# The first norm of a hybrid RWKV-7 and pooling trunk: x transposed unscaled, the row factors applied to each projection

## The chip, the cores and the metric

The kernel runs on one core of one Trainium2 chip. TensorE multiplies matrices, VectorE and ScalarE work on tiles of 128 rows, GpSimd does small things beside them, and each has its own queue of instructions that is worked off in order. SyncE issues most of the transfers from and to device memory. Matrix products land in PSUM, from where VectorE or ScalarE read them; everything else lies in SBUF. The metric is device time in microseconds (us), lower is better.

## The reference

There is one layer (DEPTH 1), a sequence of 512 rows and a width of 2048. Cut to what matters here:

```
def rms_norm(x, g):
    y = xf * lax.rsqrt(jnp.mean(xf * xf, axis=-1, keepdims=True) + RMS_EPS)
    return (y * g).astype(x.dtype)

h = rms_norm(x, norm_g[i])
z = jnp.einsum('btd,dn->btn', h, w_in[i])
zs, g_rwkv, u, g_pool = split(z)              # r, k, v, two LoRA inputs | gate | pool input | pool gate
zs = zs + (token_shift(zs) - zs) * mu[i]
w_loglog = -softplus(-(w0[i] + tanh(wd) @ w_up[i])) - 0.5
a = sigmoid(a0[i] + ad @ a_up[i])
y = wkv7_scan(rh, wh, kh, vh, kk, ah)         # the recurrence, 16 heads of 64
y_rwkv = (head_group_norm(y, ln_w, ln_b) + bonus) * silu(g_rwkv)
y_pool = (causal_multiscale_pool(u) @ w_pool) * pool_scale * silu(g_pool)
x = x + concat(y_rwkv, y_pool) @ w_out[i]
x = x + sigmoid(x @ w_pg[i] + b_pg[i]) * (p[i] @ w_ple[i])
return rms_norm(x, final_g)
```

The norm divides each row (each position of the sequence) by a factor of its own and multiplies each column by norm_g. Since the projection is linear, a row's factor may be applied to x or to the row of z.

## The kernel before, in words

Activations are kept transposed: hhi and hlo hold h with the 2048 columns on 16 groups of 128 partitions and the 512 positions along the free axis. All large products are made three times, from a high part and a low part of each operand (`mm3`: high weight with high h, high weight with low h, low weight with high h); a weight chunk of 4 times 128 rows by 128 columns comes in as `raw` (256 KB) and is split by ScalarE (`whi`, L132) and VectorE (`wlo`, L133). A projection of 128 columns (`zcols`) is 48 such products of 512 columns into one PSUM accumulator, of which there are two (`psA`).

The start loads x in row groups of 128: the first two in four pieces each, the third and fourth in halves with the LoRA columns' four weight chunks between them (`LORD`). `stats` squares a row group on ScalarE (L256) and VectorE (L258), takes the root, and multiplies x by it in place (L267, L269). Then `xt_half` transposes two row groups of one group of 128 columns at a time into PSUM (L285) and evicts the result twice: hhi by ScalarE (L286), hlo by VectorE (L287), both with norm_g as the column's factor. That goes over 16 groups of columns for positions 0 to 255, then again for 256 to 511, with the products of `z_half` for zl, the LoRA columns, between the second. WPOS and SPOS say behind which of the groups the LoRA weights are split and the later row groups are normed.

From `pin[0] = True` on TensorE keeps the order in which the program is written. Behind the start come zk, zr, zv and zg of the first head pair. For each of eight head pairs there follow its preparation (scores pm, masked by VectorE at L623) and its recurrence, `recur`: 8 chunks of three steps each, py, pu and ps. py waits for sbd (VectorE, L807 and L809), pu for zs (VectorE, L787), ps for uv (ScalarE, L797). Between the steps `pump` puts 6, 9 and 9 products of the next pair's projections or of the pool's (zb), so that TensorE has work while the other engines answer. VectorE's order is not written out: a scheduler decides it, and zs and sbd have a raised priority in it.

zl goes into `shifted` (L369 and L370) and becomes la, which is copied twice (`dup`, by transfers) and split; `decay_and_rate` multiplies it with the two LoRA matrices of each pair. silu2 (L373 and L374) makes the gates; `pool_unit` copies each pool input out of PSUM (L412). In the names below, `xt` is x, `zk`, `zr`, `zg`, `zb` are accumulators of projections, `bk` and `bkn` come from k, and `prm` holds the small parameters.

Of the kernel before, what the change touches and what calls it, by code (L numbers as in the profile page):

```python
# [9 lines left out]
F32 = mybir.dt.float32  # L10
# [24 lines left out]
def trunk_kernel(ctx: ExitStack, tc: tile.TileContext, x, p, norm_g, w_in, mu, w0, w_up, a0, a_up,  # L35
# [17 lines left out]
    psX = sx.enter_context(tc.tile_pool(name="psX", bufs=3, space=PSUM))  # L53
    xs = []

    def load_x(tt, parts):
        xt = xp.tile([P, D], F32, name=f"xt{tt}", tag="xt")
        w_ = D // parts
        for i in range(parts):
            nc.sync.dma_start(out=xt[:, i * w_:(i + 1) * w_], in_=x[tt * P:(tt + 1) * P, i * w_:(i + 1) * w_])  # L60
        xs.append(xt)
# [168 lines left out]
    def load_l():  # L230
# [2 lines left out]
        nc.sync.dma_start(out=raw, in_=src)  # L233
        lraw.append(raw)

    for step in LORD:
        if step == "l":
            load_l()
        else:
            load_x(step, 2)  # L240
# [6 lines left out]
    WPOS, SPOS = (5, 7, 9, 11), (5, 10)  # L247

    def stats(tt, parts=2):
        w_ = D // parts  # L250
        ss = xp.tile([P, parts], F32, name=f"ss{tt}", tag="ss")
        for i in range(parts):
            cs = slice(i * w_, (i + 1) * w_)
            junk = xp.tile([P, w_], F32, name=f"junk{tt}_{i}", tag=f"junk{i % 2}", bufs=2)
            if i % 2 == 0:
                nc.scalar.activation(junk, xs[tt][:, cs], AF.Square, accum_out=ss[:, i:i + 1])  # L256
            else:
                nc.vector.scalar_tensor_tensor(junk, xs[tt][:, cs], 1.0, xs[tt][:, cs], ALU.mult, ALU.mult,  # L258
                                               accum_out=ss[:, i:i + 1])
        rs = xp.tile([P, 1], F32, name=f"rs{tt}", tag="rs")  # L260
        nc.vector.tensor_reduce(rs, ss, mybir.AxisListType.X, ALU.add)
        nc.scalar.activation(rs, rs, AF.Sqrt, bias=epsr, scale=1.0 / D)
        nc.vector.reciprocal(rs, rs)
        for i in range(4):
            cs = slice(i * D // 4, (i + 1) * D // 4)
            if i % 2 == 1:
                nc.scalar.activation(xs[tt][:, cs], xs[tt][:, cs], AF.Copy, scale=rs)  # L267
            else:
                nc.vector.tensor_scalar(xs[tt][:, cs], xs[tt][:, cs], rs, None, ALU.mult)  # L269

    stats(0, 4)
# [23 lines left out]
    wl_ = []  # L295
    for d in range(KT):
        xt_half(0, d)
        if d in WPOS:
            c = len(wl_)
            wh = wp.tile([P, CK, P], F32R, name=f"whi_l_{c}", tag="whi")  # L300
            wl = wp.tile([P, CK, P], F32R, name=f"wlo_l_{c}", tag="wlo")
            split(wh, wl, lraw[c])
            wl_.append((wh, wl))
        if d in SPOS:
            stats(2 + SPOS.index(d))
    for d in range(KT):
        xt_half(1, d)
        z_half(0, d)
    for d in range(KT):
        z_half(1, d)  # L310
    pt = psM.tile([P, T], F32, name="pt_prm", tag="m")
    nc.tensor.transpose(pt[:, :nr], prow, ident[:nr, :nr])
    nc.vector.tensor_copy(prm, pt[:, :nr])
    sx.close()

# [29 lines left out]
    pin[0] = True  # L345
    wab = {}

    def load_ab(j):
# [14 lines left out]
    nc.gpsimd.memset(uaz[0][64:128, :].bitcast(F32), 0.0)  # L363
    nc.gpsimd.memset(uaz[1][0:64, :].bitcast(F32), 0.0)
    for t_ in sbd + zsp:
        nc.gpsimd.memset(t_, 0.0)

# [11 lines left out]
    lal = rw.tile([P, T], F32R, name="lal")  # L379
    hh = []  # L380
    for nm, rows in (("u", slice(0, 64)), ("a", slice(64, 128))):
        dup = rw.tile([P, T], F32, name=f"dup_{nm}", tag="t", bufs=4)
        for h in range(2):
            nc.scalar.dma_start(out=dup[64 * h:64 * h + 64, :], in_=la[rows, :])
        t_ = rw.tile([P, T], F32R, name=f"{nm}hh")
        nc.scalar.copy(t_, dup)
        nc.vector.tensor_tensor(lal[rows, :], dup[rows, :], t_[rows, :].bitcast(F32), ALU.subtract)
        hh.append(t_)
    uhh, ahh = hh

# [2 lines left out]

    place = [0]

    def zcols(ps, nm):
        for c in range(KT // CK):
            wh, wl = chunk(nm, c)
            for k in range(CK):
                kk = c * CK + k  # L400
                mm3(ps, wh[:, k, :], wl[:, k, :], hhi[:, kk, :], hlo[:, kk, :], kk == 0, kk == KT - 1)
                place[0] = 3 * (kk + 1)
                yield 3

    def pool_unit(n):
        g, i = n // 4, n % 2
        win = WINDOWS[g]
        ps = psA.tile([P, T], F32, name=f"zb{n}", tag="acc")
        yield from zcols(ps, f"b{n}")
# [51 lines left out]
    def stream():  # L461
        for kind, nm, j in jobs:
# [6 lines left out]
            if kind == "p":  # L469
# [49 lines left out]
    def decay_and_rate(j):  # L519

        (ur, us), (ar_, as_) = wab.pop(j)
        for raw, st, z_, lo, hi in ((ur, us, uaz[0], slice(64, 128), slice(0, 64)),
                                    (ar_, as_, uaz[1], slice(0, 64), slice(64, 128))):
# [6 lines left out]
        mm(ps, uaz[0], lal, start=False, stop=True)  # L530
# [650 lines left out]
```

## Time and profile before

| what | value |
| --- | --- |
| time, median of 3 runs | 1096.56 us (1095.4 to 1097.19) |
| span of the profiled execution | 1095.9 us (the page gives no time of it beside the span) |
| TensorE busy | 1070.8 us, 98% of the span |
| TensorE weight loads | 877.6 us, 80% |
| VectorE busy | 708.2 us, 65% |
| ScalarE busy | 448.3 us, 41% |
| GpSimd busy | 76.9 us, 7% |
| mean granted clock | 0.998 of full speed |
| HBM read, written | 118.02 MB, 18.87 MB; 125 GB/s over the span |

The page's strip of 40 slices has TensorE at 9 or more tenths in all slices but the first (5) and the last (6), and VectorE between 5 and 9 until about the 25th slice. A busy TensorE leaves little that a change elsewhere can win, so the stretch ahead of its first full slice, and the few waits behind it, are what the rows below look at.

### The profile page before, as it was taken

To read this page: it belongs to the slowest core of one execution; us is meant where nothing else is said; L and a number is where in the kernel's file an instruction comes from. 1 tells how busy PE (TensorE), PEld (TensorE's weight loads), DVE (VectorE), ACT (ScalarE), POOL (GpSimd) and SP (SyncE) were. 2 spreads that over 40 slices of the span, in tenths; PEclk is the share of its full clock that TensorE was granted. 3 is DMA by queue.
4 is the path that set the end of the run, shared out by engine and by line. 5 is a ranking of instruction groups with operands and counts; after the bars stand their busy time and mean duration, and the time that the engine had idled before them with its cause. 6 is when DMAs were issued, how large, how long until landed. Compare 5 with 4: busy or idle time off the path is not lost.

```text
span 1095.9 us, 17196 instructions
## 1 busy us (share of the span) xinstructions
PE 1070.8 (98%) x6060; PEld 877.6 (80%) x6060; DVE 708.2 (65%) x1835; ACT 448.3 (41%) x917; POOL 76.9 (7%) x180
## 2 busy tenths in 40 slices
PE   5999999999999999999999999999999999999996
PEld 4888878887788888788878788888888888888885
DVE  6687867878688679678886956454433424445366
ACT  7633535345335335353343344543222222233337
POOL 2100110110110110100101101000000000000000
PEclk9999999999999999999999999999999999999999
DMA  7433433332423333333334242775534438455534
GB/s 233 116 96 97 111 92 84 96 100 73 120 82 105 104 92 89 96 82 93 91 94 119 79 138 93 232 233 169 172 124 136 167 99 244 137 189 137 181 106 154
DMA packets 178486, 138.56 MB, mean 126 GB/s; under 512 B 34678, under 2 KB 139743, under 8 KB 178399
## 3 DMA queue, kind: packets, MB, share of 16 engines
q1 hardware_dynamic: 157694, 103.89, 32.1%
q10 hardware_dynamic: 20704, 33.56, 9.8%
q8 instruction: 48, 0.79, 0.3%
q14 instruction: 40, 0.32, 0.1%
HBM read 118.02 MB, written 18.87 MB: 125 GB/s over the span
## 4 chain that ended last, share of the span: by engine, by line
PE 86%; DVE 5%; DMA 4%; ACT 3%; issue 1%; SPq 0%; ACTq 0%; DVEq 0%
PE acc_o L157 16%; PE zb L157 14%; PE acc_g L157 14%; PE zv L157 8%; PE zk L157 7%; PE zg L157 7%; PE zr L157 7%; PE py L157 2%; PE pple L157 2%; PE pm L157 1%; PE pu L157 1%; DMA n<-nd 1%; PE pp L157 1%; DMA raw_g<-in_w_pg_dram 1%; PE ps L157 1%
## 5 line engine op out<-in xcount | busy, mean ns | idle before, releaser
L133 DVE TENSOR_TENSOR wlo_g<-raw_g,whi_g 128x512 fp32r<-128x512 f32 x84 | 57.0, 685 | 79.6 <-ACT whi_g L132 76.5
L157 PE MATMUL zb<-hhi,whi_b 128*128 128x512 f32 x256 | 107.0, 418 | 0.0
L133 DVE TENSOR_TENSOR wlo_o<-raw_o,whi_o 128x512 fp32r<-128x512 f32 x64 | 43.9, 690 | 91.4 <-ACT whi_o L132 91.4
L157 PE MATMUL zb<-hhi,wlo_b 128*128 128x512 f32 x256 | 100.5, 393 | 0.0
L157 PE MATMUL acc_o<-whi_o,ylo 128*128 128x512 f32 x256 | 100.2, 391 | 0.0
L157 PE MATMUL acc_o<-whi_o,yhi 128*128 128x512 f32 x256 | 99.9, 390 | 0.0
L157 PE MATMUL zb<-hlo,whi_b 128*128 128x512 f32 x256 | 99.9, 390 | 0.0
L157 PE MATMUL acc_o<-wlo_o,yhi 128*128 128x512 f32 x256 | 99.8, 390 | 0.0
L132 ACT CAST whi_g<-raw_g 128x512 fp32r<-128x512 f32 x84 | 51.9, 620 | 102.7 <-PE acc_g L157 55.4
L157 PE MATMUL acc_g<-whi_g,x2hi 128*128 128x512 f32 x208 | 81.3, 391 | 0.0
L157 PE MATMUL acc_g<-wlo_g,x2hi 128*128 128x512 f32 x208 | 80.9, 389 | 0.0
L157 PE MATMUL acc_g<-whi_g,x2lo 128*128 128x512 f32 x208 | 80.7, 389 | 0.0
L132 ACT CAST whi_o<-raw_o 128x512 fp32r<-128x512 f32 x64 | 39.9, 623 | 97.0 <-PE acc_o L157 96.7
L816 POOL TENSOR_SCALAR s0p<-sbd,pw 64x64 f32<-64x64 f32 x96 | 56.6, 589 | 322.8 <-DVE sbd L809 255.0
L132 ACT CAST whi_b<-raw_b 128x512 fp32r<-128x512 f32 x64 | 39.7, 621 | 86.5 <-PE zv L157 35.4
L133 DVE TENSOR_TENSOR wlo_b<-raw_b,whi_b 128x512 fp32r<-128x512 f32 x64 | 43.8, 685 | 34.2 <-ACT whi_b L132 32.9
L157 PEld LDWEIGHTS zb<-hhi,wlo_b 128*128 128x128 f32 x256 | 48.0, 188 | 11.1
L661 DVE TENSOR_TENSOR xw<-xw,tm 128x60 f32<-128x60 f32 (+24 forms) x248 | 52.1, 210 | 6.8
L157 PEld LDWEIGHTS acc_o<-wlo_o,yhi 128*128 128x128 f32 x256 | 48.1, 188 | 10.3 <-DVE wlo_o L133 0.4
L157 PEld LDWEIGHTS acc_o<-whi_o,yhi 128*128 128x128 f32 x256 | 48.1, 188 | 9.7
L157 PEld LDWEIGHTS acc_o<-whi_o,ylo 128*128 128x128 f32 x256 | 48.1, 188 | 9.8
L157 PEld LDWEIGHTS zb<-hhi,whi_b 128*128 128x128 f32 x256 | 48.2, 188 | 8.5
(285 smaller groups left out, 2550.0 us busy)
## 6 DMA issues: line engine op xcount, KB each, us to landing
raw_b<-in_w_in_dram SPq DMA_DIRECT2D x64, 256.0 KB
raw_o<-in_w_out_dram SPq DMA_DIRECT2D x64, 256.0 KB
raw_g<-in_w_pg_dram SPq DMA_DIRECT2D x64, 256.0 KB
raw_k<-in_w_in_dram SPq DMA_DIRECT2D x32, 256.0 KB
raw_r<-in_w_in_dram SPq DMA_DIRECT2D x32, 256.0 KB
raw_v<-in_w_in_dram SPq DMA_DIRECT2D x32, 256.0 KB
raw_g<-in_w_in_dram SPq DMA_DIRECT2D x32, 256.0 KB
n<-nd SPq DMA_DIRECT2D x16, 256.0 KB
```

Of the source, the lines that this page charges most:

```text
L132: nc.scalar.copy(hi, raw)
L133: nc.vector.tensor_tensor(lo, raw, hi.bitcast(F32), ALU.subtract)
L157: i = nc.tensor.matmul(*a, **k)
L661: nc.vector.tensor_tensor(xw[:, 0:n_, s + 1:32], xw[:, 0:n_, s + 1:32], tm[:, 0:n_, 0:w_], ALU.add)
L816: nc.gpsimd.tensor_scalar(s0p[hc, :], nxt[hc, hc], pcn[hc], None, ALU.mult)
```

## The change

The row factors no longer multiply x. x is transposed as it lands, the squares are taken beside, and the factors of all 512 positions are laid out as one row repeated over 128 partitions: four diagonal tiles (`dg`) are multiplied by a tile of ones in one fp32 product, and the result (`rsB`, 128x512) multiplies each finished projection in PSUM (`by_row`). The first two weight chunks of zk are multiplied ahead of that product (`k_first`). The loads of x come in another order, and the low parts of the LoRA operands are packed into the unused halves of their tiles.

```diff
-    load_x(0, 4)
+    load_x(0, 0)
     ngr = xp.tile([KT, P], F32, name="ngr", bufs=1)
-    load_x(1, 4)
+    load_x(1, 0)
+    for i in range(1, 4):
+        for tt in range(2):
+            load_x(tt, i)
...
-    LORD = (2, "l", "l", "l", "l", 3)
+    LORD = ("l", 2, 3, "l", 2, 3, "l", "l")
...
-        nc.vector.reciprocal(rs, rs)
-        for i in range(4):
-            cs = slice(i * D // 4, (i + 1) * D // 4)
-            if i % 2 == 1:
-                nc.scalar.activation(xs[tt][:, cs], xs[tt][:, cs], AF.Copy, scale=rs)
-            else:
-                nc.vector.tensor_scalar(xs[tt][:, cs], xs[tt][:, cs], rs, None, ALU.mult)
+    def roots():
+        rs = xp.tile([P, NT, 1], F32, name="rs", bufs=1)
+        nc.vector.tensor_reduce(rs, ssq_, mybir.AxisListType.X, ALU.add)
+        nc.scalar.activation(rs, rs, AF.Sqrt, bias=epsr, scale=1.0 / D)
+        nc.vector.reciprocal(rs, rs)
+        dg = xp.tile([P, NT, P], F32, name="dg", bufs=1)
+        for tt in range(NT):
+            nc.vector.tensor_scalar(dg[:, tt, :], ident, rs[:, tt, :], None, ALU.mult)
+        ps = psM.tile([P, T], F32, name="prs", tag="m")
+        mm(ps, ones, dg.rearrange("p a t -> p (a t)"), start=True, stop=True)
+        nc.scalar.copy(rsB, ps)
...
+    BEGUN = 2
+
+    def k_first(c):
+        wh, wl = ready.pop(("k0", c))
+        for k in range(CK):
+            kk = c * CK + k
+            mm3(begun, wh[:, k, :], wl[:, k, :], hhi[:, kk, :], hlo[:, kk, :], kk == 0, False)
...
     for d in range(KT):
         xt_half(1, d)
+        if d in (1, 5):
+            split_l()
         z_half(0, d)
     for d in range(KT):
         z_half(1, d)
+        if d % CK == CK - 1 and d < 3 * CK:
+            ahead_k()
+        square(d // 4, d % 4)
+    pin[0] = True
+    begun = psA.tile([P, T], F32, name="zk0", tag="acc")
+    for c in range(BEGUN):
+        k_first(c)
+    roots()
...
+    nc.vector.tensor_tensor(zl, zl, rsB, ALU.mult)
     shifted(zl, la, 24)
...
+    def by_row(ps):
+        nc.vector.tensor_tensor(ps, ps, rsB, ALU.mult)
...
                 place[0] = 3 * (kk + 1)
+                if kk == KT - 1 and scaled:
+                    by_row(ps)
                 yield 3
...
-            nc.scalar.copy(u_, ps)
+            nc.vector.tensor_tensor(u_, ps, rsB, ALU.mult)
...
-            nc.scalar.copy(z_[hi, :], raw[hi, :])
-            nc.vector.tensor_tensor(st[lo, :], raw[lo, :], st[lo, :].bitcast(F32), ALU.subtract)
+            nc.vector.tensor_tensor(z_[0:64, :], raw[0:64, :], st[0:64, :].bitcast(F32), ALU.subtract)
```

The first place where the order of the instructions differs is the head of VectorE's queue. Before, it reads as follows (xt_78 is the first group of 128 rows of x, xt_85 the second):

```order
L258 SCALAR_TENSOR_TENSOR junk_1_164,ss_161<-xt_78 128x512
L258 SCALAR_TENSOR_TENSOR junk_3_168,ss_161<-xt_78 128x512
L261 TENSOR_REDUCE rs_170<-ss_161 128x1
L263 RECIPROCAL rs_170<-rs_170 128x1
L269 TENSOR_SCALAR xt_78<-xt_78,rs_170 128x512 x2
L258 SCALAR_TENSOR_TENSOR junk_1_184,ss_181<-xt_85 128x512
L86 CAST blk<-blkf 128x128
L274 COPY ngc<-pt_prm 128x16
L258 SCALAR_TENSOR_TENSOR junk_3_188,ss_181<-xt_85 128x512
L261 TENSOR_REDUCE rs_190<-ss_181 128x1
L263 RECIPROCAL rs_190<-rs_190 128x1
L269 TENSOR_SCALAR xt_85<-xt_85,rs_190 128x512 x2
```

Behind these rows stood the first hlo. In the changed kernel the head of the same queue is this (xt_79 is now the second group of rows; the number behind junk is the quarter of the columns):

```order
L264 SCALAR_TENSOR_TENSOR junk_1_401,ssq__164<-xt_78 128x512
L89 CAST blk<-blkf 128x128
L281 COPY ngc<-pt_prm 128x16
L264 SCALAR_TENSOR_TENSOR junk_3_417,ssq__164<-xt_78 128x512
L264 SCALAR_TENSOR_TENSOR junk_1_427,ssq__164<-xt_79 128x512
L293 SCALAR_TENSOR_TENSOR hlo<-pt_h_0_169,ngc,hhi 128x256
L293 SCALAR_TENSOR_TENSOR hlo<-pt_h_1_174,ngc,hhi 128x256
```

The scalings and roots are gone from the head of the queue, three squares are left ahead of the first hlo.

The second place is TensorE's order between zl and zk. Before, it goes from the last products of zl (and the transposition of the small parameters, prow) to zk:

```order
L157 MATMUL zl<-hlo,whi_l_297 128x256
L157 MATMUL zl<-hhi,wlo_l_298 128x256
L312 MATMUL pt_prm<-ident,prow 128x89
L157 MATMUL zk_595<-hhi,whi_k_0_598 128x512
L157 MATMUL zk_595<-hlo,whi_k_0_598 128x512
```

In the changed kernel the first 24 products of zk stand behind zl, and then, in the middle of zk, the product that makes the row factors (prs):

```order
L163 MATMUL zk_491<-hhi,whi_k_1_439 128x512
L163 MATMUL zk_491<-hlo,whi_k_1_439 128x512
L163 MATMUL zk_491<-hhi,wlo_k_1_440 128x512
L163 MATMUL prs<-dg,ones 128x512
L167 MATMUL pt_prm<-ident,prow 128x89
L163 MATMUL zk_491<-hhi,whi_k_2_465 128x512
```

The transposition of prow moved behind the half of zk, together with prs.

The third place is VectorE's order in the recurrence of the fourth head pair. Before, zs stands behind small steps of a triangular inverse (tm and xw) and ahead of a weight's split:

```order
L661 TENSOR_TENSOR xw4_4761<-xw4_4761,tm4_4762 128x2x27
L657 TENSOR_TENSOR tm4_4762<-xw4_4761,n324_0_4666 128x2x26
L661 TENSOR_TENSOR xw4_4761<-xw4_4761,tm4_4762 128x2x26
L787 TENSOR_TENSOR zs1_569<-py3_0_4568,mv3_4382 64x128
L133 TENSOR_TENSOR wlo_r5_3_2672<-raw_r5_3_2669,whi_r5_3_2671 128x512
```

In the changed kernel the multiplication of the finished projection zk of the sixth pair stands there, and the split behind it:

```order
L688 TENSOR_TENSOR tm4_4750<-xw4_4749,n324_0_4653 128x2x26
L692 TENSOR_TENSOR xw4_4749<-xw4_4749,tm4_4750 128x2x26
L425 TENSOR_TENSOR zk5_4687<-zk5_4687,rsB_112 128x512
L139 TENSOR_TENSOR wlo_r5_3_2716<-raw_r5_3_2713,whi_r5_3_2715 128x512
L818 TENSOR_TENSOR zs1_600<-py3_0_4555,mv3_4368 64x128
```

The multiplication and the split have come ahead of zs, which stood ahead of the split before.

## Rows read from the trace of the kernel before

**Rows 1.** Stretches: bounds, length, busy (count) of five engines, clock, DMA share, GB/s
```profile
10.00:20.00 10.00, 7.66 (x42) 5.96 (x43) 8.12 (x23) 8.90 (x22) 0.00 (x0) 1.00 0.90 291
20.00:30.00 10.00, 8.85 (x67) 7.63 (x67) 9.66 (x25) 9.77 (x24) 0.00 (x0) 1.00 0.38 110
...
400.00:500.00 100.00, 99.13 (x698) 79.99 (x696) 80.84 (x241) 46.03 (x99) 9.36 (x17) 1.00 0.33 90
```
**Rows 2.** Scalings, 0 to 36 us, by form: operation and count | busy, mean ns | idle before
```profile
L269 DVE TENSOR_SCALAR xt<-xt,rs 128x512 f32<-128x512 f32 x8 | 3.5, 483 | 0.1
```
**Rows 3.** VectorE's timeline, 0 to 75 us: start, length, instruction [idle before]
```profile
6.76 0.69 DVE L258 SCALAR_TENSOR_TENSOR junk<-xt 128x512 f32<-128x512 f32 x1 [1.08 <-DMA xt<-in_x_dram]
...
10.55 0.69 DVE L258 SCALAR_TENSOR_TENSOR junk<-xt 128x512 f32<-128x512 f32 x1 [0.54 <-DMA xt<-in_x_dram]
...
13.80 2.44 DVE L287 SCALAR_TENSOR_TENSOR hlo<-pt_h,ngc,hhi 128x256 fp32r<-128x256 f32 x6 [0.84 <-ACT hhi L286]
...
26.25 7.22 DVE L287 SCALAR_TENSOR_TENSOR hlo<-pt_h,ngc,hhi 128x256 fp32r<-128x256 f32 x18
...
39.49 0.75 DVE L370 SCALAR_TENSOR_TENSOR la<-zl,prm,la 128x511 f32<-128x511 f32 x1 [1.43 <-ACT la L369]
...
72.89 0.68 DVE L600 TENSOR_TENSOR bk<-kk,ipw 128x512 f32<-128x512 f32 x1
```
**Rows 4.** TensorE's timeline, 30 to 76 us
```profile
31.63 0.38 PE L285 MATMUL pt_h<-ident,xt 128*128 128x128 f32 x2
...
35.83 0.48 PE L157 MATMUL zk<-hhi,whi_k 128*128 128x512 f32 x1
...
46.82 0.39 PE L157 MATMUL zr<-hhi,whi_r 128*128 128x512 f32 x1
...
75.47 2.06 PE L157 MATMUL pm<-ar,bk 64*128 64x128 f32 x32
```
**Rows 5.** ScalarE's timeline, 0 to 75 us (ACTq issues transfers)
```profile
9.96 0.63 ACT L256 ACTIVATE junk<-xt 128x512 f32<-128x512 f32 x1
...
36.23 1.20 ACTq L354 DMA_DIRECT2D ur<-in_w_up_dram  x2
```
**Rows 6.** TensorE's timeline, six steps of the recurrence
```profile
137.94 0.38 PE L157 MATMUL py<-sbd,ar 128*128 128x128 f32 x2
...
140.15 0.49 PE L157 MATMUL pu<-zs,x 128*128 128x128 f32 x2 [0.44 <-DVE zs L787]
...
144.85 0.38 PE L157 MATMUL py<-sbd,ar 128*128 128x128 f32 x2
...
146.46 0.38 PE L157 MATMUL pu<-zs,x 128*128 128x128 f32 x2
...
148.76 0.38 PE L157 MATMUL ps<-uv,bkn 128*128 128x128 f32 x2
...
151.06 0.38 PE L157 MATMUL py<-sbd,ar 128*128 128x128 f32 x2
```
**Rows 7.** What TensorE waited for, 36 us to the end: us, times, longest
```profile
PE py L157 <- DVE sbd L809: 1.6, 4, 0.9
PE pss L157 <- ACT bkn L700: 0.9, 2, 0.5
...
PE pu L157 <- DVE zs L787: 0.4, 1, 0.4
```
**Rows 8.** All engines, 364.9 to 367 us: one step py to pu
```profile
364.98 0.38 PE L157 MATMUL py<-sbd,ar 128*128 128x128 f32 x2
...
366.36 0.42 PEld L157 LDWEIGHTS pu<-zs,x 128*128 128x128 f32 x2
```
**Rows 9.** VectorE and ScalarE by form, 36 to 700 and to 720 us
```profile
L623 DVE TENSOR_TENSOR mt<-pm,msk 128x512 f32<-128x512 f32 x32 | 19.9, 682 | 0.9 <-PE pm L157 0.8
L133 DVE TENSOR_TENSOR wlo_b<-raw_b,whi_b 128x512 fp32r<-128x512 f32 x58 | 39.6, 685 | 27.6 <-ACT whi_b L132 26.3 <-DMA nd<-mt 0.9 <-issue 0.2
...
L412 ACT COPY u<-zb 128x512 f32<-128x512 f32 x8 | 4.7, 586 | 0.1
```

More of the change, by code (lines that the diff above doesn't have):

```diff
@@ L54, in trunk_kernel, with load_x @@
     xs = []
-    def load_x(tt, parts):
-        xt = xp.tile([P, D], F32, name=f"xt{tt}", tag="xt")
+    for tt in range(NT):
+        xs.append(xp.tile([P, D], F32, name=f"xt{tt}", tag="xt"))
+    def load_x(tt, i, parts=4):
         w_ = D // parts
-        for i in range(parts):
-            nc.sync.dma_start(out=xt[:, i * w_:(i + 1) * w_], in_=x[tt * P:(tt + 1) * P, i * w_:(i + 1) * w_])
-        xs.append(xt)
-    load_x(0, 4)
+        nc.sync.dma_start(out=xs[tt][:, i * w_:(i + 1) * w_], in_=x[tt * P:(tt + 1) * P, i * w_:(i + 1) * w_])
+    load_x(0, 0)
     ngr = xp.tile([KT, P], F32, name="ngr", bufs=1)
     nc.sync.dma_start(out=ngr, in_=norm_g[0].rearrange("(r c) -> r c", c=P))
-    load_x(1, 4)
+    load_x(1, 0)
+    for i in range(1, 4):
+        for tt in range(2):
+            load_x(tt, i)
     epsr = cst.tile([P, 1], F32, name="epsr")
@@ L90, in trunk_kernel @@
     nc.gpsimd.memset(seg.rearrange("p (c t) -> p c t", t=C)[:, :, 0:1], 0.0)
+    ones = xp.tile([P, P], F32, name="ones", bufs=1)
+    nc.gpsimd.memset(ones, 1.0)
+    rsB = cst.tile([P, T], F32, name="rsB")
     msk = cst.tile([P, 3, C], F32, name="msk")
@@ L234, in load_l @@
         lraw.append(raw)
+    halves = []
     for step in LORD:
@@ L239, in trunk_kernel @@
         else:
-            load_x(step, 2)
+            load_x(step, halves.count(step), 2)
+            halves.append(step)
     for n_, src, r_ in names:
@@ L244, in trunk_kernel @@
         nc.sync.dma_start(out=prow[col[n_]:col[n_] + r_, :], in_=flat.rearrange("(r c) -> r c", c=P))
[L247 to L256, printed above, removed]
-            else:
[L258 to L261, printed above, removed]
+    WPOS = (9, 11, 13, 15)
@@ new lines, in trunk_kernel, with square @@
+    ssq_ = xp.tile([P, NT, 4], F32, name="ssq_", bufs=1)
+    def square(tt, i):
+        cs = slice(i * D // 4, (i + 1) * D // 4)
+        junk = xp.tile([P, D // 4], F32, name=f"junk{tt}_{i}", tag=f"junk{i % 2}", bufs=2)
+        if i % 2 == 0:
+            nc.scalar.activation(junk, xs[tt][:, cs], AF.Square, accum_out=ssq_[:, tt, i:i + 1])
+        else:
+            nc.vector.scalar_tensor_tensor(junk, xs[tt][:, cs], 1.0, xs[tt][:, cs], ALU.mult, ALU.mult,
+                                           accum_out=ssq_[:, tt, i:i + 1])
@@ L271, in trunk_kernel @@
-    stats(0, 4)
+        dg = xp.tile([P, NT, P], F32, name="dg", bufs=1)
+        for tt in range(NT):
+            nc.vector.tensor_scalar(dg[:, tt, :], ident, rs[:, tt, :], None, ALU.mult)
+        ps = psM.tile([P, T], F32, name="prs", tag="m")
+        mm(ps, ones, dg.rearrange("p a t -> p (a t)"), start=True, stop=True)
+        nc.scalar.copy(rsB, ps)
     pt = psM.tile([P, T], F32, name="pt_prm", tag="m")
@@ L295, in trunk_kernel, with ahead_k, split_l @@
     wl_ = []
+    BEGUN = 2
[4 more added lines that the diff above has]
+            mm3(begun, wh[:, k, :], wl[:, k, :], hhi[:, kk, :], hlo[:, kk, :], kk == 0, False)
+    def ahead_k():
+        n_, c_, src, kt, w_ = plan.pop(0)
+        ready[n_, c_] = wsplit(src, kt, w_, f"{n_}_{c_}")
+    def split_l():
+        c = len(wl_)
+        wh = wp.tile([P, CK, P], F32R, name=f"whi_l_{c}", tag="whi")
+        wl = wp.tile([P, CK, P], F32R, name=f"wlo_l_{c}", tag="wlo")
+        split(wh, wl, lraw[c])
+        wl_.append((wh, wl))
     for d in range(KT):
         xt_half(0, d)
[L298 to L305, printed above, removed]
+        if d in WPOS[:2]:
+            split_l()
     for d in range(KT):
         xt_half(1, d)
+        if d in (1, 5):
+            split_l()
         z_half(0, d)
@@ L310, in trunk_kernel @@
         z_half(1, d)
+        if d % CK == CK - 1 and d < 3 * CK:
[6 more added lines that the diff above has]
+    roots()
     pt = psM.tile([P, T], F32, name="pt_prm", tag="m")
-    nc.tensor.transpose(pt[:, :nr], prow, ident[:nr, :nr])
+    tr(pt[:, :nr], prow, ident[:nr, :nr])
     nc.vector.tensor_copy(prm, pt[:, :nr])
@@ L343, in trunk_kernel @@
     psY = s2a.enter_context(tc.tile_pool(name="psY", bufs=2, space=PSUM))
-    pin[0] = True
     wab = {}
@@ L362, in trunk_kernel @@
     uaz = [rw.tile([P, P], F32R, name=f"uaz{i}") for i in range(2)]
-    nc.gpsimd.memset(uaz[0][64:128, :].bitcast(F32), 0.0)
-    nc.gpsimd.memset(uaz[1][0:64, :].bitcast(F32), 0.0)
+    for t_ in uaz:
+        nc.gpsimd.memset(t_[64:128, :].bitcast(F32), 0.0)
     for t_ in sbd + zsp:
@@ L386, in trunk_kernel @@
         nc.scalar.copy(t_, dup)
-        nc.vector.tensor_tensor(lal[rows, :], dup[rows, :], t_[rows, :].bitcast(F32), ALU.subtract)
+        nc.vector.tensor_tensor(t_[64:128, :], dup[64:128, :], t_[64:128, :].bitcast(F32), ALU.subtract)
         hh.append(t_)
@@ L394, in trunk_kernel, with zcols @@
     place = [0]
-    def zcols(ps, nm):
-        for c in range(KT // CK):
+    def by_row(ps):
+        nc.vector.tensor_tensor(ps, ps, rsB, ALU.mult)
+    def zcols(ps, nm, scaled=True):
+        for c in range(BEGUN if nm == "k0" else 0, KT // CK):
             wh, wl = chunk(nm, c)
@@ L408, in pool_unit @@
         ps = psA.tile([P, T], F32, name=f"zb{n}", tag="acc")
-        yield from zcols(ps, f"b{n}")
+        yield from zcols(ps, f"b{n}", n % 4 >= 2)
         if n % 4 < 2:
             u_ = pp.tile([P, T], F32, name=f"u{n}", tag="u")
-            nc.scalar.copy(u_, ps)
+            nc.vector.tensor_tensor(u_, ps, rsB, ALU.mult)
             s_ = u_
@@ L479, in stream @@
                 continue
-            ps = psA.tile([P, T], F32, name=f"z{nm}{j}", tag="acc")
+            ps = begun if (nm, j) == ("k", 0) else psA.tile([P, T], F32, name=f"z{nm}{j}", tag="acc")
             yield from zcols(ps, f"{nm}{j}")
@@ L521, in decay_and_rate @@
         (ur, us), (ar_, as_) = wab.pop(j)
[L522 to L523 removed]
+        for raw, st, z_ in ((ur, us, uaz[0]), (ar_, as_, uaz[1])):
             nc.scalar.copy(st, raw)
[L525 to L526 removed]
+            nc.vector.tensor_tensor(z_[0:64, :], raw[0:64, :], st[0:64, :].bitcast(F32), ALU.subtract)
         ps = psM.tile([P, T], F32, name=f"pu{j}", tag="m")
         mm(ps, us, uhh, start=True, stop=False)
[L530 removed]
+        mm(ps, uaz[0], uhh, start=False, stop=True)
         sig = rw.tile([P, T], F32, name=f"sig{j}", tag="t", bufs=4)
@@ L544, in decay_and_rate @@
         mm(ps, as_, ahh, start=True, stop=False)
-        mm(ps, uaz[1], lal, start=False, stop=True)
+        mm(ps, uaz[1], ahh, start=False, stop=True)
         tha = rw.tile([P, T], F32, name=f"tha{j}", tag="tha")
```

3 lines of the change are left out of this document (removed).

## The prediction

> **What bounds the kernel now.** I read the table of stretches first [rows 1]. [...] Before 30 us TensorE is the one that waits: busy 7.66 of 10 us and then 8.85 of 10, while VectorE is busy 9.66 of 10 between 20 and 30 us. So the second view is VectorE's own order of work in the start [rows 2, 3]. From 13.80 us to 33.47 (26.25 + 7.22) it has no gap worth a term, and most of what it does is the second half (hlo) of the eviction of the transposed x. TensorE goes from zl, the low-rank columns, to zk, the first full projection, at 35.83 us, and to zr at 46.82 [rows 4]. From there the products follow each other, so what counts for the end is the time at which zr starts, plus what TensorE waits for later. For that I read single steps of the recurrence [rows 6, 8] and the table of what TensorE waited for [rows 7]: there are few such waits now, each a VectorE or ScalarE result.
>
> **Start, removed.** 32 evictions cost VectorE 7.22 / 18 = 0.401 us each, 12.84 in all, and 4 splits of the LoRA weights some 0.60 each (0.685 for a split, less the 0.08 by which such rows overlap), 2.4 in all [rows 3, 9]. These 15.2 us stay. The rest of 33.47 - 13.80 = 19.67 is squares and scalings of rows 256 to 511 of x, some 4.4 us, and it leaves this stretch: the scalings (0.48 each [rows 2], four of the eight here) go altogether, and the squares now stand behind the evictions.
>
> **Start, when VectorE begins.** The change does not let the evictions start with the first piece of x. In VectorE's new order three squares stand ahead of the first hlo, in ScalarE's four ahead of the first hhi. The second of VectorE's is on the last quarter of the first 128 rows, which is now the eighth transfer in the queue. The eighth before (third quarter of the next 128 rows) had landed when ScalarE squared it at 9.96, the ninth at 10.55 [rows 3, 5]. So I take 9.96 + 2 x 0.69 = 11.34 for the start of the evictions. It cannot be much earlier: the fourth transfer was there at 6.76 [rows 3], and eight of them by the queue's pace come to about 9.6.
>
> **Start, sum.** 11.34 + 12.84 + 2.4 = 26.6, with some 0.3 of small waits 26.9, against 33.47. TensorE follows later than that: the last pair of transposes needs the PSUM tile of six evictions earlier, 26.9 - 6 x 0.401 = 24.5, ends at 24.6, and behind it stand 48 products of zl at 0.12 us each (before, 35 stood between the last transpose at 31.63 and zk at 35.83: 4.20 / 35) [rows 4]. 24.6 + 5.76 = 30.4 for zk, 5.4 earlier than 35.83.
>
> **Added: the row factors.** After 24 of the 48 products of zk (10.99 / 48 = 0.229 us each [rows 4], 5.5 in all, so at 35.9) TensorE makes the row factors with one fp32 product of 512 columns. VectorE has them ready by about 34.1, if it does the remaining squares, two splits of zk's weights, reduce, reciprocal and four diagonal tiles from 26.9 on; 1.8 us to spare, so no wait. The trace has no fp32 product of that width. Upper bound: an fp32 product of 128 columns adds 151.06 - 148.76 = 2.30, less nine products of 0.227, = 0.26 to a step [rows 6], four times that is 1.06. Lower bound: two ordinary rows of 512 columns, 0.45. I take 1.0, next to the row of its own kind. zr then starts at 30.4 + 11.0 + 1.0 = 42.4, against 46.82: 4.4 us gained at this point.
>
> **Added: 32 multiplications of projections, 8 of gates, 1 of zl; 8 moved from ScalarE.** 49 VectorE instructions on 128x512. The trace has none that writes into PSUM; with PSUM read and SBUF written one takes 0.682, with SBUF alone 0.685 [rows 9]. I take 0.68 each, 33 us in all. Between 400 and 500 us VectorE is busy 80.84 of 100 [rows 1], and 33 us over some 650 us is 5 more in a hundred. So VectorE isn't filled; what matters is which instruction waits behind a multiplication in VectorE's order.
> [...]
>
> **What waits behind them.** By the new order 24 multiplications stand directly, or with one split of a weight between, ahead of zs or sbd, the two VectorE steps of the recurrence that TensorE waits for. A step from py to pu is 146.46 - 144.85 = 1.61 us, the other two 2.30 [rows 6]. In nine places ahead of sbd, 0.60 of a multiplication (0.68 less 0.08 overlap) and 0.60 of a split end 1.87 us into a step that gives 2.07: no wait. Six stand directly ahead: no wait. In nine places of the later recurrences it reads multiplication, split, zs. There the projection ends as py does; multiplication to 0.65, split to 1.25, zs 0.28 more, done at 1.55 to 1.60, and the weight load for pu wants it 1.38 after py (366.36 - 364.98) [rows 8]. The trace shows what a late zs costs: 140.15 - 137.94 = 2.21, that is 0.60 more than 1.61 [rows 6]. I take 0.15 each, 1.4 in all. Bounds: nothing (the step absorbs it as the weight load is short), and 24 x 0.6 = 14.4 if each place costs what that one did. I take the low one since the waits of before are few and of 0.4 to 0.9 [rows 7].
> For the first pair, bk has three more VectorE instructions ahead of it (2.1 us), and the scores wait for it at 75.47 with 1.9 us to spare (72.89 + 0.68 = 73.57) [rows 3, 4]; TensorE itself comes 4.4 earlier. Since VectorE's chain from zk comes earlier by as much, the term is 0.2.
> ScalarE loses 16 small copies and 8 of 0.586 [rows 9]; it is not what TensorE waits for except in two waits of 0.9 in sum [rows 7], of which I count 0.2 back. The decay products change their operands, not their number: nothing.
>
> **Sum.** -5.4 + 1.0 + 0.2 + 1.4 - 0.2 = -3.0. The profile gives the execution's span, 1095.9, and no time around it; the median of the three runs, 1096.56, is 0.66 above it. 1095.9 - 3.0 + 0.66 = 1093.6. As a case by itself it spans 1092.2 to 1095.2: 0.5 either way from the fp32 product and the landing of x, 1 from the waits.
>
> **Rivals.**
> - *zr waits for zl's buffer.* There are two such accumulators; zr needs the one that zl leaves. zl can be multiplied only when the row factors are copied (36.9 + 0.59, a copy of that shape [rows 9]), then 0.68, and ScalarE, which in its order first issues four transfers (1.20 us for two [rows 5], 2.4), reaches its own reading of zl at about 40, VectorE's follows to 41.3; zr comes at 42.4. Before, zl was left at 39.49 + 0.75 = 40.24 [rows 3], 6.6 ahead of zr. If roots or that queue are over 1.1 late, every microsecond more is one of TensorE's. With 1.5 to 2.5 lost: 1095.1 to 1096.1.
> - *The multiplications hold the recurrence up.* Same mechanism as the 1.4 above, at a higher price: at the 24 places TensorE waits for zs or sbd. It turns the gain into a loss from (5.4 - 1.0) / 24 = 0.18 us per place. At 0.3: 7.2, less the 4.4 gained, 1096.56 + 2.8 = 1099.4. For it: the one wait of 0.60. Against it: 15 of the 24 places have room by the steps' own lengths.
> - *More gain.* The waits that are there now (1.6 + 0.9 + 0.4 [rows 7]) go in part, because other instructions stand at those places, and the fp32 product costs 0.45: 1.5 to 2.5 less, 1091.1 to 1092.1.
> - *It does not do what it says*, if the evictions still began no earlier than 13.8: 26.9 becomes 29.4, the gain falls by 2.5, 1096.1.
>
> **Chances.** Forecast 0.58; zr's buffer 0.12; the recurrence held up 0.18; more gain 0.08; no earlier start 0.04. A measurement of this kernel can tell about 0.2%, 2.2 us, from no change: faster is below 1094.4, slower above 1098.8. Of the forecast's 0.58 some 0.43 lie below 1094.4; with "more gain" 0.51 faster. The rest of the forecast, the buffer, the late start and the part of the recurrence rival under 0.2 us per place make 0.33 the same. Slower 0.16. The range reaches down to the lower end of "more gain", and up to where the recurrence rival stands at 0.25 per place (1098.2).
>
> **What would show it.** Right: first hlo near 11.3, no scaling of x, last hlo near 27; zk near 30.4, zr near 42.4; in the table of TensorE's waits some nine new short ones on zs, under 0.3 each; multiplications at 0.68. Wrong: TensorE idle before zr or before the row factors' product; waits on zs or sbd of several us in sum; a multiplication that takes clearly longer with PSUM on both sides; transposes that start late for want of x.

## The result and the profile after

The changed kernel takes 1101.95 us (median of 4 runs, 1101.39 to 1103.56), the kernel before 1096.55 us beside it. The ratio is 1.0046 with a 95% interval of 1.0032 to 1.0061: 5.4 us slower, where 3 us faster was forecast, and 3.8 us above the forecast's upper end.

The span of the profiled execution is 1099.7 us; its own time is 1101.39, 1.7 more. That difference is 1.7 to 1.8 us in the profiled execution of every later run. By it the profile of before (span 1095.9) came from an execution of about 1097.6 us, an estimate, one above its median; so the spans differ by 3.8 us where the times differ by 5.4. One of the nine executions of a later run (e10) took 5464 us and is left out of its ratio.

First the start. VectorE's timeline after the change (columns as in [rows 3], idle time in brackets):

```profile
10.82 0.69 DVE L264 SCALAR_TENSOR_TENSOR junk<-xt 128x512 f32<-128x512 f32 x1 [3.76 <-DMA xt<-in_x_dram]
...
12.05 1.26 DVE L293 SCALAR_TENSOR_TENSOR hlo<-pt_h,ngc,hhi 128x256 fp32r<-128x256 f32 x3
...
18.01 0.69 DVE L144 TENSOR_TENSOR wlo_l<-raw_l,whi_l 128x512 fp32r<-128x512 f32 x1 [0.39 <-ACT whi_l L143]
...
22.00 0.69 DVE L144 TENSOR_TENSOR wlo_l<-raw_l,whi_l 128x512 fp32r<-128x512 f32 x1 [0.95 <-ACT whi_l L143]
...
24.78 4.23 DVE L293 SCALAR_TENSOR_TENSOR hlo<-pt_h,ngc,hhi 128x256 fp32r<-128x256 f32 x10
```

The evictions begin at 12.05 instead of 13.80 [rows 3] and end at 29.01 instead of 33.47. The first row is the square of x that VectorE's queue holds ahead of them; the two waits are on ScalarE. TensorE's timeline shows what that gives:

```profile
27.02 0.38 PE L291 MATMUL pt_h<-ident,xt 128*128 128x128 f32 x2
...
32.98 0.40 PE L163 MATMUL zk<-hhi,whi_k 128*128 128x512 f32 x1
...
38.45 1.02 PE L163 MATMUL prs<-dg,ones 128*128 128x512 f32 x2
...
39.33 0.48 PE L163 MATMUL zk<-hhi,whi_k 128*128 128x512 f32 x1
...
44.88 0.39 PE L163 MATMUL zr<-hhi,whi_r 128*128 128x512 f32 x1
```

zk starts 2.85 us earlier than in [rows 4], zr 1.94 earlier: the fp32 product took 0.88 of it (38.45 to 39.33). So the start gained, but less than half of what was forecast. All the rest is loss behind it. What TensorE waited for from 30 us on (engine, line, releaser: us, times, longest), to be held against [rows 7]:

```profile
PE py L163 <- DVE sbd L840: 4.8, 5, 1.7
PE px L163 <- issue: 1.4, 2, 0.7
PE pu L163 <- DVE zs L818: 1.3, 3, 0.7
PE pss L163 <- ACT bkn L731: 0.8, 3, 0.4
```

The waits on sbd have gone from 1.6 to 4.8 us, those on zs from 0.4 to 1.3, and px, which did not wait, now does. One of them in full, VectorE and TensorE together, a step py of the first pair's recurrence:

```profile
148.56 0.19 DVE L688 TENSOR_TENSOR tm<-i,n 128x31 f32<-128x31 f32 x1 [3.82 <-DMA n<-nd]
...
150.83 0.70 DVE L425 TENSOR_TENSOR zg<-zg,rsB 128x512 f32<-128x512 f32 x1
151.44 0.59 DVE L840 SCALAR_TENSOR_TENSOR sbd<-ps,pw,s0p 64x64 f32<-64x64 f32 x2
...
152.09 0.49 PE L163 MATMUL py<-sbd,ar 128*128 128x128 f32 x2 [1.69 <-DVE sbd L840]
```

The same py in the kernel before is the last row of [rows 6], at 151.06 with no wait, and VectorE stood there like this:

```profile
147.90 0.19 DVE L657 TENSOR_TENSOR tm<-i,n 128x31 f32<-128x31 f32 x1 [2.33 <-DMA n<-nd]
...
150.18 0.60 DVE L809 SCALAR_TENSOR_TENSOR sbd<-ps,pw,s0p 64x64 f32<-64x64 f32 x2
```

Two things stand ahead of sbd in VectorE's queue and add up. The first instruction of the inverse (tm) waits for a transfer that goes out to device memory and back; the steps behind it then run without a gap up to sbd. This was so before, and sbd came just in time. The multiplication of zg is 0.6 us more in that chain. The start, 1.94 us earlier at zr, does not help: tm came 0.66 us later than before. Of the 1.69 us the multiplication is thus the smaller part. The transfer is the larger: tm began 9.9 us after the last of its writes to device memory had been issued (at 138.67), where it had been 8.4 us in the kernel before and is 7.5 in e1 below, which has none of these multiplications. Why the way took longer is not shown.

The other waits on sbd are of two kinds (the same timeline, later):

```profile
452.26 0.70 DVE L425 TENSOR_TENSOR zk<-zk,rsB 128x512 f32<-128x512 f32 x1
...
454.11 0.49 PE L163 MATMUL py<-sbd,ar 128*128 128x128 f32 x2 [1.06 <-DVE sbd L840]
...
606.00 0.67 DVE L139 TENSOR_TENSOR wlo_b<-raw_b,whi_b 128x512 fp32r<-128x512 f32 x1
606.71 0.29 DVE L840 SCALAR_TENSOR_TENSOR sbd<-ps,pw,s0p 64x64 f32<-64x64 f32 x1
...
607.05 0.49 PE L163 MATMUL py<-sbd,ar 128*128 128x128 f32 x2 [1.29 <-DVE sbd L840]
```

Ahead of 454.11 and of a short wait at 626.93 a multiplication and a split stand before sbd, as at 152.09. Ahead of 607.05 and of 302.32 (0.57 us) no multiplication does: the inverse's steps and a weight's split do, as in the kernel before.

The multiplications themselves are as long as forecast (0.68). What was not forecast is the column behind the second bar, VectorE's idle time directly ahead of them (three of the six groups):

```profile
L425 DVE TENSOR_TENSOR zg<-zg,rsB 128x512 f32<-128x512 f32 x8 | 5.6, 699 | 7.1 <-PE zg L163 7.0
...
L425 DVE TENSOR_TENSOR zk<-zk,rsB 128x512 f32<-128x512 f32 x8 | 5.6, 698 | 3.9 <-PE zk L163 3.8
...
L445 DVE TENSOR_TENSOR u<-zb,rsB 128x512 f32<-128x512 f32 x8 | 5.5, 689 | 3.5 <-PE zb L163 3.5
```

Over all six groups that is 24.3 us in which VectorE stood before a multiplication whose projection was not finished. Idle time of VectorE is not yet a loss, since what stands behind the multiplication may not be wanted sooner. Of TensorE's waits on sbd and zs only one lies behind such a stand:

```profile
522.98 0.70 DVE L425 TENSOR_TENSOR zk<-zk,rsB 128x512 f32<-128x512 f32 x1 [1.32 <-PE zk L163]
...
524.78 0.49 PE L163 MATMUL pu<-zs,x 128*128 128x128 f32 x2 [0.23 <-DVE zs L818]
```

In the kernel before ScalarE was the first to read a projection, and VectorE's reading of it (L370, L374) has 0.1 to 0.2 us of such idle time in each group. And ScalarE, the first reader then, now waits in its turn. Its timeline at the first px that waits:

```profile
122.11 0.36 ACT L776 COPY q<-pq 32x256 f32<-32x256 f32 x1 [2.32 <-PE pq L163]
122.66 0.69 ACT L397 ACTIVATE sv<-zv,dprm 128x512 f32<-128x512 f32 x1 [0.19 <-DVE zv L425]
123.25 0.61 ACT L138 CAST whi_g<-raw_g 128x512 fp32r<-128x512 f32 x1
123.88 0.36 ACT L776 COPY q<-pq 32x256 f32<-32x256 f32 x1
```

px needs both copies of q. Before, sv<-zv ran at 120.63 and the two copies together from 123.05; now it comes between them, because it waits for the multiplication of zv, and the second copy starts 1.41 us after the first is done (122.47 to 123.88). The waits table calls this "issue", so the name of a releaser is not enough: one has to look at the queue of the engine that makes the operand.

### The profile page after: what moved, and what is told of

It is laid out like the page before. It is cut to its first block, busy times and chain, and to the rows that moved or that the text cites. A ratio compares the mean times of both kernels' runs of the same rounds, so it can differ in the third digit from the quotient of the medians.

```text
span 1099.7 us, 17211 instructions
## 1 busy us (share of the span) xinstructions
PE 1072.3 (98%) x6062; PEld 878.7 (80%) x6062; DVE 733.5 (67%) x1878; ACT 436.3 (40%) x887; POOL 73.1 (7%) x181
## 4 chain that ended last, share of the span: by engine, by line
PE 88%; DVE 6%; DMA 2%; ACT 2%; issue 2%; SPq 0%; ACTq 0%; DVEq 0%
PE acc_o L163 16%; PE acc_g L163 16%; PE zb L163 14%; PE zr L163 7%; PE zv L163 7%; PE zk L163 7%; PE zg L163 7%; PE pple L163 2%; PE py L163 2%; PE pu L163 2%; DMA n<-nd 1%; PE pm L163 1%; PE pp L163 1%; PE zl L163 1%; PE ps L163 1%
## 5 line engine op out<-in xcount | busy, mean ns | idle before, releaser
L139 DVE TENSOR_TENSOR wlo_g<-raw_g,whi_g 128x512 fp32r<-128x512 f32 x84 | 56.7, 683 | 77.4 <-ACT whi_g L138 77.4
L139 DVE TENSOR_TENSOR wlo_o<-raw_o,whi_o 128x512 fp32r<-128x512 f32 x64 | 43.8, 690 | 89.9 <-ACT whi_o L138 89.9
L139 DVE TENSOR_TENSOR wlo_b<-raw_b,whi_b 128x512 fp32r<-128x512 f32 x64 | 43.6, 683 | 22.5 <-ACT whi_b L138 21.6
```

The costliest lines, as they stand in the source:

```text
L139: nc.vector.tensor_tensor(lo, raw, hi.bitcast(F32), ALU.subtract)
```

## The experiments

Theory A: the multiplications stand in VectorE's order ahead of zs and sbd, and TensorE waits. Theory B: the loss is of another part (the start, the packing, the phase of the inverse's transfer), and the multiplications are hidden. To compare the same place across kernels, this is by how many us an instruction of TensorE starts later (+) or earlier (-) than in the kernel before; the column heads are its start there:

```
kernel                        zr 46.82  px 124.47  py 151.06  pu 392.39  py 450.81  py 601.95  pu 698.51
after                           -1.94     -0.13      +1.03      +1.64      +3.30      +5.10      +5.44
e1, no multiplications          -1.92     -1.90      -1.88      -2.69      -2.80      -2.40      -2.40
e2, before + multiplications    +0.31     +2.18      +4.22      +6.30      +8.17      +8.54      +8.86
e3, multiplications late        -1.45     +0.59      -0.11      +2.17      +2.81      +5.16      +5.39
e4, squares last                -2.29     +0.05      +1.45      +3.16      +4.62      +6.36      +6.69
e5, e4 and splits held          -3.94     -2.20      -1.39      -0.09      +1.56      +2.68      +3.06
e6, after, inverse later        -0.96     +1.04      +0.34      -0.76      -0.40      -0.24      +0.23
e7, before, inverse later       -0.10     +0.12      +0.13      -2.15      -2.62      -3.47      -3.57
e9, e3 + e5 + e6                -3.22     -1.59      -2.28      -0.83      -1.44      +1.87      +1.76
e10, e5 + e6                    -4.43     -2.13      -2.84      -3.95      -3.56      -3.43      -3.01
e11, e7 and packing             -0.40     -0.40      -0.39      -2.97      -3.57      -4.67      -4.76
```

Each row is a single execution, and not always a typical one. The row of e3 is the slowest of its twelve (1101.51 us, median 1098.89), the row of e9 the fastest (1097.87, median 1101.15). The granted clock counts too: from 30 us to the last 10 it is 1.00 in all these traces but four. In e2 TensorE stood 2.59 us before a py at 155.28, and over 155 to 160 us the granted clock is 0.66; that is (1 - 0.66) x 5 = 1.7 us of TensorE's time, an estimate. e4 (behind a wait of 1.93 us at 152.51) and e3 (behind 1.78 at 302.62) lose 1.7 us each in the same way, and e9 twice that (the mean clock of these four executions is 0.996, 0.996, 0.997 and 0.995, where the kernel before has 0.998). The later columns of these four rows hold it. Behind the wait of 1.69 us in the changed kernel's trace the clock stayed at 1.00; that execution has a mean of 0.998, but two of the four have 0.996, so a part of its loss may be of this kind too.

**e1: the change without the multiplications.**

```diff
-                if kk == KT - 1 and scaled:
-                    by_row(ps)
...
-            nc.vector.tensor_tensor(u_, ps, rsB, ALU.mult)
+            nc.scalar.copy(u_, ps)
```

> The changed kernel without the 32 multiplications of projections and the 8 of pool gates and inputs (the inputs copied by ScalarE as before); only zl is still multiplied. The result is therefore unscaled. Theory A (the multiplications stand in VectorE's queue ahead of zs and sbd and TensorE waits for them): the recurrence is as before, the start's gain of 2 us stays, 1094.0 to 1096.0, and the waits on zs and sbd fall from 6.1 us to about 2. Theory B (the start, the packing of the decay's low parts and the phase in which the transfers of the inverse come back make the loss; the multiplications are hidden): 1099 or more.

1094.25 us; ratio to before 0.9971 (0.9961 to 0.9981). The waits:

```profile
PE py L163 <- DVE sbd L838: 1.6, 5, 0.4
PE pu L163 <- DVE zs L816: 0.4, 1, 0.4
PE pss L163 <- ACT bkn L729: 0.4, 2, 0.2
```

The waits on sbd and zs are those of [rows 7] again and px does not wait. Between the changed kernel (1.0046) and this one (0.9971) lie 0.75%, 8 us, for 48 VectorE instructions (L425 x40, L445 x8). At the last pu of the table it is 7.8.

**e2: the kernel before with the multiplications, by a tile of ones.**

```diff
+    rsB = cst.tile([P, T], F32, name="rsB")
+    nc.gpsimd.memset(rsB, 1.0)
...
+                if kk == KT - 1 and scaled:
+                    by_row(ps)
```

(and the packing of the change, to make room for the tile.)

> The kernel before, with its own start and scaling of x, but with the same 40 multiplications, by a tile of ones, and with the decay's low parts packed as in the change (which makes room for the tile). Theory A: the loss without the gain, 1102 to 1104, with waits on zs and sbd of 5 us or more. Theory B: within 1.5 us of before, 1095 to 1098.

1103.5 us, ratio 1.0051 (1.0033 to 1.0069). With the start, the scaling of x and the loads of before, the loss is there, 5.6 us where it is 8 with the new start. Two rows of its waits are

```profile
PE py L159 <- DVE sbd L813: 4.5, 4, 2.6
...
PE pu L159 <- DVE zs L791: 1.4, 3, 0.7
```

Together e1 and e2 show that the multiplications cost the loss, with either start, and exclude B as it was put. That they do it only by standing ahead of zs and sbd, as theory A has it, they do not show: the waits on px are ScalarE's, and the transfer came back later with the multiplications than without.

**e3: the multiplications behind the next zs or sbd.** In the recurrence a finished projection's multiplication and its readers are kept in a list and traced behind the next of the two in VectorE's queue.

```diff
         def step():
             hop[0] += 1
+            if lead[0] is not None:
+                with tc.issue_after(lead[0].ins):
+                    settle()
```

> The changed kernel; in the recurrence a finished projection is multiplied and read only behind the next zs or sbd in VectorE's queue (the pool's inputs too; the pool's gates stay). Same work, another place. Theory A: most of the waits go, 1095 to 1097.5. Theory B: no change, 1101 to 1103. A third way: the multiplications cost VectorE time wherever they stand, because what is behind them (splits of weights, the inverse) comes late instead: 1099 to 1101.

1098.89 us, ratio 1.0011 (0.9999 to 1.0022): some 3.8 us better than the change by the ratios. That is between theory A (up to 1097.5) and the third way (from 1099). The stall at 151.06 is gone (-0.11 in the table), but its trace, of its slowest execution, still has 5.0 us of waits on sbd, elsewhere. At those places no multiplication stands directly ahead; the inverse's steps and a weight's split do. Whether the multiplication earlier in the step or the inverse's transfer made them late, this run alone does not tell (e6 and e9 below do for the transfer).

**e4 and e5: the start.** e4 puts the squares behind the evictions; e5 also holds the splits of the LoRA weights at their places.

```diff
-        square(d // 4, d % 4)
+        with tc.issue_after(ev[d % 2].ins):
+            square(d // 4, d % 4)
...
+        with tc.issue_after(ev[0].ins), tc.issue_after(ev[1].ins):     # e5
             split(wh, wl, lraw[c])
```

> The changed kernel with all sixteen squares behind the evictions on both engines, nothing else. If the squares at the head of the two queues and among the evictions kept the start from gaining what was forecast: first hlo at 6 to 7 us instead of 12.05, zk at 28 to 30 instead of 32.98, zr at 40 to 42 instead of 44.88, and the time 3 to 4 us less, about 1098 to 1099. If instead the arrival of x sets it: zk no earlier than 32 and the time 1101 to 1103. If the row factors then come late: TensorE idle ahead of the fp32 product, gain about 1.

> The changed kernel with the squares behind the evictions (as in e4) and the four splits of the LoRA weights held at the places where the program has them, so that no split stands ahead of evictions that are ready. In e4 ScalarE stood 5.28 us before a split whose weights had not landed. Theory of the start: hlo from 6.3 on with no wait over 1 us before the second half, last hlo at 21 to 24 (28.25 in e4), zk at 27 to 29, zr at 39 to 41 (44.88 in the changed kernel), time 3 to 5 us less, 1097 to 1099. Rival: the second half of x and the last weights, which land at 18 us or later, hold the second half, so that zk moves by less than 2. A third way: the row factors come too late for their product, since sixteen squares now follow the last hlo; then zr gains 2 less than zk.

e4: 1103.03 us, ratio 1.0043 (1.0026 to 1.006), no gain; zk came at 32.62 and zr at 44.53. The first hlo came at 6.29, and then ScalarE's queue stopped at a split whose weights, now tenth in the queue of transfers, had not landed:

```profile
12.38 0.62 ACT L143 CAST whi_l<-raw_l 128x512 fp32r<-128x512 f32 x1 [5.28 <-DMA raw_l<-in_w_in_dram]
```

e5: 1099.76 us, ratio 1.0027 (1.0017 to 1.0038); zk at 30.97, zr at 42.88, some 2 us better than the change, where 3 to 5 were expected. The rival was half right: the second split still waited 2.10 us for its weights, and the last hlo came at 26.6, not at 21 to 24. zk and zr are thus near the forecast's times (30.4 and 42.4), but by luck: the forecast's evictions were to begin at 11.3 and run without a gap, those of e5 begin at 6.41 and lose some five us in waits on ScalarE, which waits for x and for weights.

**e6 and e7: the inverse two steps later**, on the change and on the kernel before.

```diff
-    HS, HN = 5, 2
+    HS, HN = 7, 2
```

> The changed kernel with the next pair's triangular inverse begun two steps later in the recurrence (HS 7 instead of 5), so that its first instruction, which waits for a transfer through device memory, stands behind sbd instead of ahead of it. If the loss is the sum of two things in VectorE's queue, the wait for that transfer and the multiplication behind it: waits on sbd fall from 4.8 to about 1, time 1098 to 1099.5. If the multiplication alone is the cause: within 1 us of the changed kernel, 1101 to 1103.

> The kernel before with that same later inverse and nothing else. Few waits are there to remove (1.6 us on sbd): 1095 to 1097.5, at most 1.5 less than before. If it were 3 less, the gain in e6 would not be about the multiplications at all.

e6: 1096.2 us, ratio 0.9991 (0.9982 to 1.0); e7: 1092.77 us, ratio 0.9956 (0.9941 to 0.997). The waits of e6, then those of e7:

```profile
PE px L163 <- issue: 1.4, 2, 0.8
PE pu L163 <- DVE zs L818: 1.0, 3, 0.4
PE pss L163 <- ACT bkn L731: 0.8, 3, 0.4
...
PE py L163 <- DVE sbd L840: 0.2, 1, 0.2
```

```profile
PE pss L157 <- ACT bkn L700: 0.9, 2, 0.5
PE pu L157 <- DVE zs L787: 0.4, 1, 0.4
PE py L157 <- DVE sbd L809: 0.3, 1, 0.3
```

In both the waits on sbd are nearly gone: with the tm that waits for the transfer behind sbd, the multiplication no longer makes it late. So the big sbd waits were the sum of two. But both expectations missed: e6 gained 5.8 us, more than the 2.5 to 4 expected, and e7 gained 4.4, not 1.5. A gain of 3 in e7 was to mean that e6's gain is not about the multiplications. Most of it is not: the early inverse costs the kernel before 4.4 us without them.

The table of waits had shown too little of what an early tm cost the kernel before. e7's offsets fall from +0.13 to -3.57 between 151 and 699 us, while the waits on sbd that are named in [rows 7] are 1.6. Step by step, 2.4 us of it lie in the steps from ps to py and 1.0 in those from py to pu. In the kernel before the step from the ps at 297.94 took 3.38 us, that from 312.35 took 2.78, where most take 2.30; TensorE's idle time in them is 0.92 and 0.31. A late sbd or zs lengthens a step by some 0.17 us more than the idle time that is shown.

With the later inverse the multiplications still cost: from zr to the pu at 698.51 e6 lost 1.19 us and e7 gained 3.47, 4.7 between them, or some 5.5 against e11 below, which has the packing as e6 has. With the early inverse it was 7.8 (after less e1 at that pu).

**e9: e3, e5 and e6 together.**

> The changed kernel with the three edits together: the start of e5, the multiplications behind zs or sbd as in e3, the inverse later as in e6. If each removes its own wait: about 1092 to 1094, below the kernel before by 3 to 5 us. If the multiplications still hold up what is behind them: 1095 to 1098.

1101.15 us, ratio 1.0032 (1.0022 to 1.0042): above both cases. A new wait replaces the old:

```profile
PE pq L163 <- DVE y L790: 5.4, 2, 3.1
```

VectorE's timeline ahead of the second of them:

```profile
493.92 0.68 DVE L460 TENSOR_TENSOR u<-zb,rsB 128x512 f32<-128x512 f32 x1
...
497.04 0.69 DVE L928 TENSOR_TENSOR yo<-yo,sg 128x512 f32<-128x512 f32 x1
...
497.72 0.42 DVE L790 STREAM_TRANSPOSE y<-x 32x256 f32<-32x256 f32 x1
```

Multiplication and inverse, both moved back, now meet at the end of the recurrence: the transposition of the inverse (y), on which pq depends, stands behind the pool input's late multiplication, its window sums and the pair's output (yo) in VectorE's queue. What is put off must still be done before the next thing waits for it.

The other part of the time is the clock. The granted clock ahead of the second wait and behind it:

```profile
490.00:495.00 5.00, 5.00 (x26) 3.88 (x24) 4.97 (x5) 1.53 (x3) 0.00 (x0) 1.00 0.05 7
500.00:505.00 5.00, 5.00 (x49) 3.72 (x48) 4.61 (x7) 2.25 (x7) 0.84 (x1) 0.78 0.19 54
```

(columns as in [rows 1], the clock is the third from the end.) In the profiled execution, the fastest, the mean clock is 0.995; in the other eleven it is 0.991 to 0.994, where those of e6 have 0.997 or 0.998. From 0.998 to 0.992 is some 6.6 us of 1100, an estimate. So e9 does not show that the three edits are worth nothing, only that these two waits cost more than their length.

**e10 and e11: what is left together.** e10 is e5 with the later inverse; e11 is e7 with the packing of the change.

> The changed kernel with the start of e5 and the later inverse of e6, the multiplications where the change has them. If the two gains add (2.2 us in e5, 5 to 6 in e6): 1093.5 to 1095, below the kernel before by 2 to 3.5 us, but not below e7, since the multiplications still cost the waits on px, pss and zs, some 4 us. If the earlier start only makes TensorE wait longer for the second engine's work in the first recurrences: 1096 to 1097.

> The kernel of e7 (before with the later inverse) with the one further part of the change that costs VectorE nothing: the decay's low parts packed into the free halves of their tiles, 16 small ScalarE copies fewer. Theory: they are hidden, within 1 us of e7, 1092 to 1094. If ScalarE's order mattered (its waits on pss are 0.9 us): up to 1 us less. If the packing was a part of the loss: 1 to 3 us more than e7.

e10: 1093.9 us, ratio 0.9961 (0.9947 to 0.9975): the two gains add, and the change so mended beats the kernel before by 0.4%. e11: 1091.94 us, ratio 0.9943 (0.9923 to 0.9963), the fastest of all. It scales x as the kernel before does and has no multiplication of projections. Its interval overlaps with e7's, so the packing's gain is not settled by the times; its trace is 1.2 us ahead of e7's at the last pu (-4.76 against -3.57).

## Why the prediction was wrong

- **What waits behind them** is the step that failed. It took 0.15 us for nine places ahead of zs, 1.4 in all, and nothing for fifteen places ahead of sbd. Measured, the multiplications cost 8 us by time (e1 against the change). Step by step against e1:
  - *Ahead of zs* the price was near. Eight steps from py to pu that took 1.61 us took 1.74 (three), 1.87 (three), 2.00 and 2.50: 2.4 us in all.
  - *Ahead of sbd* three steps (to the py at 152.09, 454.11 and 626.93) were 1.85, 0.78 and 0.32 us longer: 3.0 where nothing was counted. The sum for these places, 1.87 of 2.07 us, started each multiplication when ps did. Here they started 2.90, 1.67 and 0.77 us after ps, because the inverse's steps stood ahead of them, and at the first two a transfer had held these up.
  - *On ScalarE* nothing was counted either. Its copy of q behind its reading of zv is 1.4 us of waits on px; the stretches up to the two px that wait are 1.8 and 0.7 us longer than in e1.
  - The projection's last product, for which the multiplications wait, was the smaller matter: in seven of the eight zs steps the multiplication had stood idle before it, and these are 1.6 us longer together. The sbd places that cost had none.
- The rival "the multiplications hold the recurrence up" is what happened. Its price, 0.3 us at 24 places less the start's gain, gave 1099.4; it had a chance of 0.18, and its threshold of 0.18 us a place lay below the 0.44 of the one such wait that [rows 6] shows, which should have weighed more. Its mechanism, zs and sbd late, is the larger part of the loss; ScalarE's part it did not have.
- **Start, sum**: forecast -5.4 at zk and -4.4 at zr, measured -2.85 and -1.94. Landing was sized too early (the seventh piece of x was squared at 10.82, not 9.96, so 12.05 for 11.34), and ScalarE's queue was not added up: VectorE waited 0.39 and 0.95 us for its splits, the second time behind two squares that ScalarE did at 19.76 and 20.38. In e5 zk and zr came at the forecast's times, 30.97 and 42.88, by another way (see there). That an earlier start reaches the end is shown by e5 and e10.
- **The row factors**: 0.88 for the fp32 product (1.0 taken; the upper bound is 1.03 by its own rows, not 1.06); TensorE did not wait for them, the last diagonal tile was done at 36.72. Right.
- **zr waits for zl's buffer**: zl's last reading ended at 43.80, zr came at 44.88, 1.1 to spare as worked out. Right that it didn't decide.
- **The price of a multiplication**: 0.689 to 0.699 against 0.68 taken. Right. With PSUM on both sides VectorE takes 0.691 to 0.699 by group (L425), with PSUM read and SBUF written 0.689 (L445), where a split in SBUF of the same shape takes 0.672 to 0.690 (L139).

Open: why the inverse's transfer took longer at 152.09, and why a late sbd or zs lengthens a step by more than TensorE's idle time. Steps that are shorter and longer for other reasons, up to 0.9 us each, nearly cancel in the sums above; they were not taken apart.

## What to carry to other kernels

Here an instruction put into an in-order queue cost nothing where what stood behind it had room, and else its own length (0.70) or a part of it, and what held it up: 0.32, 0.78 and 1.85 us at three places ahead of sbd. So ask when it can start, what stands ahead of it, and which short, urgent instruction comes next. The idle time of the engine ahead of it is no price by itself: the steps behind the 24.3 us of it here became some 1.6 us longer in all. Before adding work to such a queue look for what already waits in it for a transfer: the two add up, and here moving the transfer's reader back two steps gained more (4.4 us) than the change without its multiplications did (3.4, e1). And when the first reading of a projection moved from ScalarE to VectorE, ScalarE had to wait (L397: 5.2 to 8.2 us in each group of eight for VectorE's multiplication), with its own queue behind it (1.4 us of TensorE's waits on px).

## What the runs showed that was not expected

The kernel before had 4.4 us in the place of one instruction that waits for a transfer, of which the waits table names 1.6. The start varies by about 1 us between executions: zr of the same start came at 44.88 (after), 44.90 (e1), 45.37 (e3) and 45.86 (e6). The arrival of x alone does not explain it: the square that waits for its seventh piece began at 10.82, 10.26, 10.80 and 11.23. And some waits cost more than their length: behind the wait of 2.59 us in e2 the granted clock is 0.66 over 155 to 160 us, behind the second of the two in e9 it is 0.78 over 500 to 505, and e9's mean of 0.995 against 0.998 is 3.3 us of 1096: some 1.7 us of TensorE's time for each of the three waits, an estimate.
